# A two-block transformer on one core: another opening, own buffers for modulation weights, bias rows in 16 copies

## The chip, the cores and the metric

One Trainium2 chip, one of its cores, one launch. The metric is the device time of the launch in microseconds (us), the median of several runs. Data lies in the device's HBM at the start; every weight is read once.

## The reference, cut to what matters

Two blocks of two layers each work on x of 256 tokens by 1024 features, all in fp32. Only the parts that the change meets are written out.

```python
def first_block(x, c, ...):
    c_act = silu(c)                                   # 1 x 1024
    for l in range(2):
        mod = c_act @ w_ada[l] + b_ada[l]             # 6 x 1024: w_ada[l] is 1024 x 6144
        sh1, sc1, gt1, sh2, sc2, gt2 = split(mod, 6)
        h = rms_norm(x, norm_mix[l]) * (1 + sc1) + sh1
        p = h @ w_in[l]                               # all projections of the mixer
        # y_att: dilated attention; y_rwkv: a linear recurrence per head (8 heads);
        # y_gmlp: spatial gating with w_s, b_s
        merged = sum over the three of sigmoid(gates) * (y @ w_branch[l])
        x = x + gt1 * (merged @ w_out[l])
        h = rms_norm(x, norm_ffn[l]) * (1 + sc2) + sh2
        x = x + gt2 * conv_gated_ffn(h, ...)          # 1024 -> 2 x 2816 -> 1024
    return rms_norm(x, norm_final)

def second_block(x, p, rel_bias, ...):                # 2 layers: ffn1, mixer, ffn2, gated p @ w_pe_proj
    # the mixer's attention adds bias = rel_bias[t5_buckets(key - query)], 8 heads, window 128
```

## The kernel before

x is kept transposed: eight tiles of 128 features by 256 tokens. Every large product is made of three matmuls on a split into a high and a low part: each weight half (`raw`, 128 x 1024, 512 KB) is read by the sync queue (SP), cast to the high part by ScalarE (L137), and VectorE takes the difference as the low part (L138). `mm3` (L164 to L166) then does high x high, high x low, low x high. A call of `wload` reads one weight pair, two halves. The weight buffers stand in rings: 3 raw and 4 split ones for the whole program, and 3 and 2 or 3 and 3 more in the opening's pool `st` and the feed-forward's pool `wx`. Activations are split likewise (`split`, L201 and L202) into 17 buffers of pool `hp`.

The opening (`build`, L1340 on, and `LayerA.__init__`, L362 on): c is loaded as one row, spread to 128 partitions by a matmul, and scaled. x comes in eight loads on the sync queue. Weight pairs 12 and 6 follow, then the modulation weights of the first shift and scale, 16 blocks of 128 outputs by 1024 (six loads of 1 MB and four halves), with pair 10 before the last four halves. Each block's product with silu(c) is one VectorE operation that multiplies and sums along the row (L371). Meanwhile `rms` sums the squares of x on VectorE (L222), reduces them by one-column matmuls (L228), takes the root and reciprocal (L240, L241) and spreads the result (L248). `modulated` makes the eight h tiles: product with the norm on VectorE (L418), scale and shift on ScalarE (L419), split. `fmulti` then runs the three first weight pairs, k outermost, for all their columns; the second column of each sits in one of only two `aux` PSUM buffers.

The other 80 modulation blocks of 512 KB (`ada_task`, L337 load, L338 product) are called from a list, 0.67 of one at each `wload` (`tick`), and take the next raw buffer of the weight ring. The results are needed at the entries of mixers and feed-forwards and before their last products.

In the first feed-forward (`ffn_a`), after 8 of 22 weight pairs, `bias_rows` (L1004 on) makes 8 rows of 512 from `rel_bias` by a matmul and writes each 128 times to HBM (`skew`, L1018, on ScalarE's DMA queue). `bias_table` (L1023) reads it back at the start of the second block, shifted by one element from row to row, in two loads on SP; the second block's attention adds it (L1050). In the first feed-forward `project` (L1261 on) also does a small product of the second block and writes it to HBM in 256 KB pieces (L1285); it has four buffers of one tag.

The recurrence runs per pair of heads (`rwkv_pair`, generators that are advanced between weight pairs); the buffer counts of its tiles are in `BUFS`. The spatial gating's weights `w_s` have a tile of their own (`ws`, L886).

The kernel is written in a tile language. Its compile-time scheduler reorders what each engine and DMA queue is given: among the instructions whose inputs, by its own cost model, are ready and whose buffers are free, the first in program order goes next. On the chip each engine and queue then works strictly in that fixed order.

Of the kernel before, what the change touches and what calls it, by code (L numbers as in the profile page):

```python
# [17 lines left out]
S = 256  # L18
D = 1024
# [31 lines left out]
class K:  # L51
    def __init__(self, tc, ctx, ins):
# [4 lines left out]
        self.hp = E(tc.tile_pool(name="hp", bufs=17))  # L57
# [274 lines left out]
def ada_task(G, l, f, mods, cact):  # L332
    def run():
        nc = G.nc
        p, b = G.ring("raw")
        raw = p.tile([128, D], F32, tag="raw", bufs=b, name=G.nm("raw"))
        nc.sync.dma_start(raw, G.ins["w_ada"][l, f // 2, :, (f % 2) * D:(f % 2) * D + D])  # L337
        nc.vector.scalar_tensor_tensor(raw, raw, 1.0, cact, MUL, MUL, accum_out=mods[f // 8][:, f % 8:f % 8 + 1])  # L338
    return run


class LayerA:


    def __init__(self, G, l, pool, cact, first=None, late=None):
# [12 lines left out]
        else:  # L358

            for n, j in enumerate((0, 4, 1, 5, 2, 6, 3, 7)):  # L360
                if n == 6:
                    late()  # L362
                raw = first.tile([128, 2, D], F32, tag="ada", bufs=8, name=G.nm("raw"))
                src = v3(G.ins["w_ada"][l, j], 2)
                if n < 6:
                    nc.sync.dma_start(raw, src)
                for h in range(2):
                    if n >= 6:
                        nc.sync.dma_start(raw[:, h, :], src[:, h, :])
                    f = 2 * j + h  # L370
                    nc.vector.scalar_tensor_tensor(raw[:, h, :], raw[:, h, :], 1.0, cact, MUL, MUL, accum_out=self.mods[f // 8][:, f % 8:f % 8 + 1])  # L371
        G.bg += [((l, f), ada_task(G, l, f, self.mods, cact)) for f in range(0 if first is None else 16, 48)]
# [66 lines left out]
BUFS = dict(P=1, iP=1, kkn=1, kp=1, BK=1, AR=2, bv=2, uv=8, SA=1, SR=2, BT=2, AT=2, Q=4, R=1, X=1, Y=1, ST=2, y=2)  # L439


def rwkv_pair(G, L, mp, p, zk, zr, zv, zwa, sg, out, O):
# [80 lines left out]
    rkb = mp.tile([128, 128], F32, tag="rkb", name=G.nm("rkb"), bufs=2)  # L523
# [211 lines left out]
def mix_a(G, L, x, l, mp, pre, dbg=None):  # L735
# [81 lines left out]
    def gmlp_bias():  # L817
        tt(ws, ws, G.c("causal", 128).unsqueeze(1).to_broadcast([128, 8, 128]), MUL)
        yield 1.5
        for p in range(4):  # L820
            ps = G.aux()
            for g in range(2):
                mm(ps[64 * g:64 * g + 64, :128], G.ones[:, :64], ws[:, 2 * p + g, :], start=True, stop=True)
# [14 lines left out]
    def gmlp_out():  # L838
        for p in range(4):
            ps = G.aux()  # L840
            for t in range(2):
                for g in range(2):
                    mm(ps[64 * g:64 * g + 64, t * 128:t * 128 + 128], gv[t][:, (2 * p + g) * 64:(2 * p + g) * 64 + 64],
                       ws[:, 2 * p + g, :], start=True, stop=True)
# [41 lines left out]
    ws = mp.tile([128, 8, 128], F32, tag="ws", name=G.nm("ws"), bufs=1)  # L886
    nc.sync.dma_start(ws, G.ins["w_s"][l])
# [5 lines left out]
    start(3)  # L893
    heads(1)
# [679 lines left out]
```

## Time and profile before

| what | value |
|---|---|
| median of 3 runs | 2295.76 us (2294.28 to 2296.1) |
| the profiled execution | 2297.13 us |
| its span, from the first to the last instruction | 2295.3 us |
| TensorE (PE) busy | 2206.4 us, 96% |
| weight loads of TensorE (PEld) | 2131.8 us, 93% |
| VectorE (DVE) | 1685.2 us, 73% |
| ScalarE (ACT) | 1286.4 us, 56% |
| read from HBM | 408.40 MB |

A view groups or lists the instructions of that one execution; times count from the span's first instruction. "PE" are matmuls, "PEld" the weight loads that overlap them, "SPq" and "ACTq" what the queues of SyncE and ScalarE issue. L12 is line 12 of the kernel. An instruction's idle time is that of its engine just before it, with who ended it. Matmuls are pipelined: their listed durations overlap, and the distance of their starts tells the pace.

### The profile page before, as it was taken

What the parts mean: (1) busy time and instruction counts of PE and PEld (TensorE: products, weight loads), DVE (VectorE), ACT (ScalarE), POOL (GpSimd) and SP (SyncE); (2) the same over time, 40 slices, a digit from 0 to 9 for tenths busy, and PEclk for the clock granted to TensorE, in tenths of its full rate; (3) what the DMA queues carried; (4) which work ended last, traced back from release to release, by engine and by line L of the source; (5) the groups of instructions that cost most, each with busy time, mean ns of one, the idle gap of its engine ahead of it and who ended that gap; (6) DMA issues with size and microseconds to landing.
All of it is one profiled execution on the core that took longest, in us unless ns stands there. A gap on an engine that the chain in (4) does not pass through costs nothing.

```text
span 2295.3 us, 46372 instructions
## 1 busy us (share of the span) xinstructions
PE 2206.4 (96%) x18850; PEld 2131.8 (93%) x18850; DVE 1685.2 (73%) x3042; ACT 1286.4 (56%) x2184; POOL 4.2 (0%) x10
## 2 busy tenths in 40 slices
PE   5999998978999999999999999999999999999999
PEld 4889998978888999899999999999999999999999
DVE  6887777757678877776576569976677656997665
ACT  4575546544557554655454466664465446665444
POOL 0000000000000000000000000000000000000000
PEclk9999999989999999999999999999999999999999
DMA  7634457777563446765675663466565556346653
GB/s 289 200 121 150 148 192 256 224 220 231 179 188 122 150 150 190 262 213 156 176 238 170 173 196 109 140 216 184 158 209 182 171 175 194 102 149 214 184 159 124
DMA packets 129148, 416.66 MB, mean 182 GB/s; under 512 B 14596, under 2 KB 20356, under 8 KB 128166
## 3 DMA queue, kind: packets, MB, share of 16 engines
q1 hardware_dynamic: 126750, 409.50, 57.0%
q10 hardware_dynamic: 2184, 4.19, 1.0%
q8 instruction: 148, 2.42, 0.4%
q14 instruction: 66, 0.54, 0.1%
HBM read 408.40 MB, written 5.24 MB: 180 GB/s over the span
## 4 chain that ended last, share of the span: by engine, by line
PE 77%; DMA 9%; DVE 7%; ACT 5%; issue 1%; SPq 0%; ACTq 0%; DVEq 0%
PE ps L164 22%; PE ps L165 22%; PE ps L166 22%; DVE lo L138 3%; DMA skew<-ohb 2%; ACT hi L137 2%; DMA raw<-in_ffn_up 2%; DMA raw<-in_w_ada 2%; DMA raw<-in_w_in 1%; PE rec L601 1%; PE rec L593 1%; DVE raw L371 1%; DMA raw<-in_w_out 1%; PE rec L1182 1%; PE aux L1044 0%
## 5 line engine op out<-in xcount | busy, mean ns | idle before, releaser
L164 PE MATMUL ps<-h,hi 128*128 128x256 f32 x5080 | 1437.1, 284 | 31.0 <-ACT h L201 28.5
L166 PE MATMUL ps<-h,lo 128*128 128x256 f32 x5080 | 1433.2, 283 | 15.4 <-DVE lo L138 15.4
L165 PE MATMUL ps<-l,hi 128*128 128x256 f32 x5080 | 1432.2, 283 | 5.1 <-DVE l L202 5.0
L137 ACT CAST hi<-raw 128x1024 fp32r<-128x1024 f32 (+1 forms) x724 | 704.8, 977 | 640.2 <-PE ps L165 360.3
L138 DVE TENSOR_TENSOR lo<-raw,hi 128x1024 fp32r<-128x1024 f32 (+1 forms) x724 | 819.7, 1134 | 300.7 <-ACT hi L137 297.6
L164 PEld LDWEIGHTS ps<-h,hi 128*128 128x128 f32 x5080 | 959.7, 189 | 44.1 <-ACT h L201 30.8
L166 PEld LDWEIGHTS ps<-h,lo 128*128 128x128 f32 x5080 | 961.2, 189 | 21.0 <-DVE lo L138 16.8
L165 PEld LDWEIGHTS ps<-l,hi 128*128 128x128 f32 x5080 | 961.2, 189 | 11.2 <-DVE l L202 6.8
L201 ACT CAST h<-t 128x256 fp32r<-128x256 f32 x172 | 68.7, 403 | 126.1 <-DVE t L1000 96.2
L202 DVE TENSOR_TENSOR l<-t,h 128x256 fp32r<-128x256 f32 x172 | 72.5, 424 | 66.1 <-ACT h L201 65.7
L338 DVE SCALAR_TENSOR_TENSOR raw<-raw,cact 128x1024 f32<-128x1024 f32 x80 | 97.4, 1218 | 30.3 <-DMA raw<-in_w_ada 30.2
L997 DVE TENSOR_TENSOR t<-ps,r 128x512 f32<-128x512 f32 x88 | 60.8, 691 | 41.6 <-PE ps L166 41.2
L1187 DVE SCALAR_TENSOR_TENSOR cy<-cp,cwh,cy 128x256 f32<-128x256 f32 x192 | 85.2, 478 | 3.2 <-ACT cy L1185 2.9
L215 ACT ACTIVATE t<-x 128x256 f32<-128x256 f32 x96 | 38.5, 407 | 16.4 <-DVE x L968 9.1
L222 DVE TENSOR_TENSOR t<-t,t 128x256 f32<-128x256 f32 x87 | 36.6, 421 | 5.4 <-ACT t L215 4.1
L190 PE MATMUL ps<-hi,h 128*128 128x256 f32 x128 | 38.2, 299 | 0.0
L191 PE MATMUL ps<-hi,l 128*128 128x256 f32 x128 | 37.7, 294 | 0.0
L1000 DVE TENSOR_TENSOR t<-t,t 128x256 f32<-128x256 f32 x88 | 36.9, 420 | 1.0 <-ACT t L999 1.0
L192 PE MATMUL ps<-lo,h 128*128 128x256 f32 x128 | 37.4, 292 | 0.0
L999 ACT ACTIVATE t<-t 128x256 f32<-128x256 f32 x88 | 36.1, 411 | 0.9
L964 ACT ACTIVATE t<-t 128x256 f32<-128x256 f32 x44 | 18.1, 415 | 27.3 <-DVE t L963 27.0
L419 ACT ACTIVATE t<-t,sh,am 128x256 f32<-128x256 f32 x32 | 18.1, 596 | 26.5 <-DVE am L398 22.5
(312 smaller groups left out, 1890.3 us busy)
## 6 DMA issues: line engine op xcount, KB each, us to landing
raw<-in_w_in SPq DMA_DIRECT2D x176, 512.0 KB, 4.3
raw<-in_ffn_in SPq DMA_DIRECT2D x176, 512.0 KB, 4.5
raw<-in_ffn_up SPq DMA_DIRECT2D x88, 512.0 KB, 5.6
raw<-in_w_ada SPq DMA_DIRECT2D x84, 512.0 KB, 4.8
raw<-in_ffn_out SPq DMA_DIRECT2D x64, 384.0 KB, 3.1
raw<-in_ffn_out SPq DMA_DIRECT2D x64, 320.0 KB, 3.2
raw<-in_w_branch SPq DMA_DIRECT2D x24, 512.0 KB, 4.2
raw<-in_ffn_down SPq DMA_DIRECT2D x32, 384.0 KB, 3.1
```

Source lines behind the costliest of these rows:

```text
L137: nc.scalar.copy(hi[:, :m], raw[:, :m])
L138: nc.vector.tensor_tensor(lo[:, :m], raw[:, :m], hi[:, :m], SUB)
L164: mm(ps, w[0], x[0], start=first, stop=False)
L165: mm(ps, w[0], x[1], start=False, stop=False)
L166: mm(ps, w[1], x[0], start=False, stop=last)
L190: mm(ps[:, :256], x[k][0][:, sl], h, start=k == 0, stop=False)
L201: nc.scalar.copy(h, src)
L202: nc.vector.tensor_tensor(l, src, h, SUB)
L215: nc.scalar.square(sq, x[k])
L338: nc.vector.scalar_tensor_tensor(raw, raw, 1.0, cact, MUL, MUL, accum_out=mods[f // 8][:, f % 8:f % 8 + 1])
L997: nc.vector.tensor_tensor(v3(gu, 2), v3(ps, 2), rb, MUL)
L1187: stt(y, cp[:, jj:jj + S], cwh[:, jj * 4 + i:jj * 4 + i + 1], y, MUL, ADD)
```

## The change

The opening: silu(c) is loaded in 128 copies and as a column; x goes out on two queues; the 16 modulation blocks come one by one, scale block k and shift block k for k from 0 to 7, five of them in another layout for TensorE (8 matmuls of one column each), with the weight pairs 12, 6 and 10 after the second, fourth and last pair of blocks; all eight squares go to TensorE, which sums them. Later blocks get two buffers of their own. A block's load and its product are tied behind the instruction traced just before them on their engine (`keep_in_program_order`), and a product is traced only when the block after the next is called, or at a `need`. `modulated` puts the shift into the split, except in the opening. The bias rows are made in 16 copies as one 128 x 512 tile and written once; the table is read in 16 loads on GpSimd's queue. There are fewer buffers in some places: one less of `hp`, one less raw of the feed-forward, fewer in the recurrence (`BUFS`, `rkb`), and `ws` now takes two buffers of the z tiles.

```diff
-        self.hp = E(tc.tile_pool(name="hp", bufs=17))
+        self.hp = E(tc.tile_pool(name="hp", bufs=16))
...
+    def ada_flush(self, keep=0):
+        while len(self.ada_pend) > keep:
+            self.ada_pend.pop(0)()
...
+    def rms_pe(self, x):
+        ps = self.aux()
+        sqs = []
+        for k in range(8):
+            sq = self.tmp(S)
+            nc.scalar.square(sq, x[k])
+            sqs.append(sq)
+        self.load_ident()
+        for t in range(2):
+            for k, a in enumerate(sqs):
+                nc.tensor.matmul(ps[:, t:t + 1], a[:, t * 128:t * 128 + 128], self.ones[:, 0:1], start=k == 0, stop=k == 7)
+        return self.spread(self.inv_rms(ps[:, :2]), False)
...
-def ada_task(G, l, f, mods, cact):
+def ada_task(G, l, f, mods, cact, pool):
     def run():
-        p, b = G.ring("raw")
-        raw = p.tile([128, D], F32, tag="raw", bufs=b, name=G.nm("raw"))
-        nc.sync.dma_start(raw, G.ins["w_ada"][l, f // 2, :, (f % 2) * D:(f % 2) * D + D])
-        nc.vector.scalar_tensor_tensor(raw, raw, 1.0, cact, MUL, MUL, accum_out=mods[f // 8][:, f % 8:f % 8 + 1])
+        G.ada_flush(ADA_BUFS - 1)
+        raw = pool.tile([128, D], F32, tag="adar", bufs=ADA_BUFS, name=G.nm("ada"))
+        G.tc.keep_in_program_order(nc.sync.dma_start(raw, G.ins["w_ada"][l, f // 2, :, (f % 2) * D:(f % 2) * D + D]))
+        def product():
+            G.tc.keep_in_program_order(
+                nc.vector.scalar_tensor_tensor(raw, raw, 1.0, cact, MUL, MUL, accum_out=mods[f // 8][:, f % 8:f % 8 + 1]))
+        G.ada_pend.append(product)
...
-            for n, j in enumerate((0, 4, 1, 5, 2, 6, 3, 7)):
...
+            for k in range(8):
+                for f in (8 + k, k):
+                    raw = first.tile([128, D], F32, tag="ada", bufs=15, name=G.nm("raw"))
+                    out = self.mods[f // 8][:, f % 8:f % 8 + 1]
+                    if f in ADA_PE:                    # 0, 1, 2, 3, 5
+                        nc.sync.dma_start(raw, G.ins["w_ada_pe"][ADA_PE.index(f)])
+                        ps = G.rec()
+                        for i in range(8):
+                            nc.tensor.matmul(ps[:, 0:1], raw[:, i * 128:i * 128 + 128], ccol[:, i:i + 1], start=i == 0, stop=i == 7)
+                        nc.scalar.copy(out, ps[:, 0:1])
+                    else:
+                        nc.sync.dma_start(raw, G.ins["w_ada"][l, f // 2, :, (f % 2) * D:(f % 2) * D + D])
+                        nc.vector.scalar_tensor_tensor(raw, raw, 1.0, cact, MUL, MUL, accum_out=out)
+                late(k)                                # k 1, 3, 7: load_w of pairs 12, 6, 10
...
 def modulated(G, x, a, sh):
-        nc.vector.tensor_tensor(t, x[k], r, MUL)
-        nc.scalar.activation(t, t, AF.Identity, scale=a[:, k:k + 1], bias=sh[:, k:k + 1])
-        out.append(G.split(t))
+            nc.vector.scalar_tensor_tensor(t, x[k], a[:, k:k + 1], r, MUL, MUL)
+            h, l = (G.hp.tile([128, S], F32R, tag="h", name=G.nm("h")) for _ in range(2))
+            nc.scalar.activation(h, t, AF.Identity, bias=sh[:, k:k + 1])
+            nc.vector.scalar_tensor_tensor(l, t, sh[:, k:k + 1], h, ADD, SUB)
...
-BUFS = dict(P=1, iP=1, kkn=1, kp=1, BK=1, AR=2, bv=2, uv=8, SA=1, SR=2, BT=2, AT=2, Q=4, R=1, X=1, Y=1, ST=2, y=2)
+BUFS = dict(P=1, iP=1, kkn=1, kp=1, BK=1, AR=2, bv=2, uv=8, SA=1, SR=2, BT=2, AT=1, Q=3, R=1, X=1, Y=1, ST=2, y=1)
...
-    ws = mp.tile([128, 8, 128], F32, tag="ws", name=G.nm("ws"), bufs=1)
-    nc.sync.dma_start(ws, G.ins["w_s"][l])
+    wst = [mp.tile([128, 2, S], F32, tag="zkr", name=G.nm("ws"), bufs=3).rearrange("p a (b j) -> p (a b) j", b=2) for _ in range(2)]
+    for i in range(2):
+        nc.sync.dma_start(wst[i], G.ins["w_s"][l][:, 4 * i:4 * i + 4, :])
...
-    sk = G.dr.tile([8, 128, 512], F32, name="skew")
-    nc.tensor.matmul(ps[0:8, :], rel, oh, start=True, stop=True)
-    t = pool.tile([8, 512], F32, tag="ohb", name="ohb")
-    nc.scalar.dma_start(sk, t.unsqueeze(1).to_broadcast([8, 128, 512]))
+    sk = G.dr.tile([128, 512], F32, name="skew")
+    rel16 = pool.tile([33, 128], F32, tag="rel16", name="rel16")
+    nc.vector.tensor_copy(v3(rel16, 16), rel.unsqueeze(1).to_broadcast([33, 16, 8]))
+    nc.tensor.matmul(ps, rel16, oh, start=True, stop=True)
+    t = pool.tile([128, 512], F32, tag="pj", name="ohb", bufs=5)
+    nc.scalar.dma_start(sk, t)
...
     for q in range(2):
-        G.nc.sync.dma_start(bias[:, :, q, :], src)
+        for a in range(0, 128, 16):
+            src = bass.AP(tensor=sk.tensor, offset=sk.offset + 127 - a + (128 if q == 0 else 0), ap=[[8 * 512 - 1, 16], [512, 8], [1, 256]])
+            G.nc.gpsimd.dma_start(bias[a:a + 16, :, q, :], src)
...
-        return mp.tile([128, 512], dt, tag=tag, name=G.nm("pj"), bufs=4)
+        return mp.tile([128, 512], dt, tag=tag, name=G.nm("pj"), bufs=5 if tag == "pj" else 4)
...
-                nc.sync.dma_start(t, ins["x"][:, k, :])
+                G.tc.keep_in_program_order((nc.scalar if k % 2 else nc.sync).dma_start(t, ins["x"][:, k, :]))
...
-                        G.weights(wx, 3, 3)
+                        G.weights(wx, 2, 3)
```

## Rows read from the trace of the kernel before

**Rows 1.** Busy time by stage: stretch, its us, each engine's busy us (instructions), PEclk, DMA share, GB/s.

```profile
0.00:56.10 56.10, 27.43 (x160) 23.53 (x161) 38.55 (x90) 25.25 (x45) 2.29 (x7) 1.00 0.81 295
56.10:370.30 314.20, 304.25 (x2915) 281.20 (x2913) 252.12 (x549) 188.19 (x347) 0.96 (x1) 1.00 0.54 171
370.30:382.40 12.10, 8.59 (x59) 8.39 (x60) 7.20 (x15) 5.80 (x11) 0.00 (x0) 0.86 0.94 319
382.40:600.40 218.00, 195.97 (x1586) 192.78 (x1587) 151.32 (x251) 104.59 (x166) 0.00 (x0) 0.95 0.72 220
600.40:954.70 354.30, 337.77 (x3130) 314.43 (x3128) 273.57 (x585) 209.61 (x386) 0.99 (x2) 0.97 0.55 171
954.70:1144.70 190.00, 189.95 (x1601) 189.62 (x1601) 131.82 (x204) 107.54 (x176) 0.00 (x0) 1.00 0.60 185
1144.70:2295.30 1150.60, 1142.41 (x9404) 1121.81 (x9403) 830.63 (x1353) 645.43 (x1059) 0.00 (x0) 1.00 0.56 173
```

**Rows 2.** The same view of the opening, its first 10 us and the rest.

```profile
0.00:10.00 10.00, 3.78 (x4) 1.16 (x4) 2.73 (x9) 6.03 (x11) 1.16 (x5) 1.00 0.64 178
10.00:45.00 35.00, 15.08 (x89) 14.21 (x90) 30.42 (x67) 13.05 (x22) 0.00 (x0) 1.00 1.02 396
```

**Rows 3.** Groups by line, opening: operation, count, busy us, mean ns, idle before.

```profile
L371 DVE SCALAR_TENSOR_TENSOR raw<-raw,cact 128x1024 f32<-128x1024 f32 x16 | 19.0, 1220 | 0.0
L138 DVE TENSOR_TENSOR lo<-raw,hi 128x1024 fp32r<-128x1024 f32 x7 | 8.5, 1223 | 5.2 <-ACT hi L137 5.2
...
L419 ACT ACTIVATE t<-t,sh,am 128x256 f32<-128x256 f32 x8 | 4.5, 595 | 22.5 <-DVE am L398 22.5
```

**Rows 4.** Timeline of TensorE in the opening: start, us, instruction, idle before it.

```profile
30.29 0.58 PE L164 MATMUL ps<-h,hi 128*128 128x256 f32 x1 [13.67 <-ACT h L201]
...
35.73 0.41 PE L164 MATMUL aux<-h,hi 128*128 128x256 f32 x1
35.95 0.34 PE L165 MATMUL aux<-l,hi 128*128 128x256 f32 x1
...
55.99 0.28 PE L166 MATMUL aux<-h,lo 128*128 128x256 f32 x1
```

**Rows 5.** The chain that ended last, 425 to 550 us: start, us, what.

```profile
435.26 47.28 DMA skew<-ohb
...
524.10 4.75 DMA raw<-in_w_ada
```

**Rows 6.** Waits of TensorE, first feed-forward: us in total, times, longest.

```profile
PE ps L166 <- DVE lo L138: 14.0, 4, 7.3
PE ps L164 <- ACT h L201: 9.8, 3, 3.5
```

**Rows 7.** Line 228 in the opening: durations min/median/max ns, first and last start.

```profile
L228 PE MATMUL aux<-ones,t x8: 352/352/373, 10.1 to 11.6; 128*128 128x1 f32 x8
```

**Rows 8.** Waits of VectorE, and of the sync queue, whole span.

```profile
DVE raw L338 <- DMA raw<-in_w_ada: 30.2, 25, 4.0
...
SPq L337 <- DVE lo L138: 116.1, 42, 11.1
```

**Rows 9.** Timeline: feed-forward's tail (VectorE, TensorE), then its entry (VectorE, ScalarE).

```profile
528.88 1.23 DVE L338 SCALAR_TENSOR_TENSOR raw<-raw,cact 128x1024 f32<-128x1024 f32 x1 [1.91 <-DMA raw<-in_w_ada]
...
539.30 0.39 PE L164 MATMUL ps<-h,hi 128*128 128x256 f32 x1 [3.16 <-ACT h L201]
...
378.38 0.42 DVE L418 TENSOR_TENSOR t<-x,aux 128x256 f32<-128x256 f32 x1 [2.02 <-PE aux L248]
...
380.48 0.59 ACT L1284 COPY pj<-ps 128x512 f32<-128x512 f32 x1 [4.10 <-DMA proj<-pj]
```

**Rows 10.** Waits of TensorE, second mixer.

```profile
PE rec L262 <- ACT t L483: 2.5, 1, 2.5
```

**Rows 11.** Lines 669 and 521 in the first mixer: first and last start.

```profile
L669 DVE SCALAR_TENSOR_TENSOR yr<-y,vec,rec x4: 479/480/481, 175.8 to 322.8; 128x256 f32<-128x256 f32 x4
...
L521 DVE TENSOR_TENSOR t<-z,kp x4: 417/418/421, 73.1 to 233.6; 128x256 f32<-128x256 f32 x4
```

**Rows 12.** Line 1050: first and last start.

```profile
L1050 DVE SCALAR_TENSOR_TENSOR sc<-aux,bias x16: 680/683/692, 1408.8 to 2013.4; 128x512 f32<-128x512 f32 x16
```

More of the change, by code (lines that the diff above doesn't have):

```diff
@@ L358, in __init__ @@
         else:
-            for n, j in enumerate((0, 4, 1, 5, 2, 6, 3, 7)):
[L361 to L372, printed above, removed]
+            for k in range(8):
[12 more added lines that the diff above has]
+                late(k)
+        G.bg += [((l, f), ada_task(G, l, f, self.mods, cact, p)) for f in range(0 if first is None else 16, 48)]
     def load_small(self):
@@ L413, in modulated @@
     nc = G.nc
-    r = G.rms(x, False, True)
+    r, first = G.first_rms, G.first_rms is not None
+    G.first_rms = None
+    if not first:
+        r = G.rms(x, False, True)
     out = []
@@ L417, in modulated @@
         t = G.tmp(S)
-        nc.vector.tensor_tensor(t, x[k], r, MUL)
-        nc.scalar.activation(t, t, AF.Identity, scale=a[:, k:k + 1], bias=sh[:, k:k + 1])
-        out.append(G.split(t))
+        if first:
+            nc.vector.tensor_tensor(t, x[k], r, MUL)
+            nc.scalar.activation(t, t, AF.Identity, scale=a[:, k:k + 1], bias=sh[:, k:k + 1])
+            out.append(G.split(t))
+        else:
+            nc.vector.scalar_tensor_tensor(t, x[k], a[:, k:k + 1], r, MUL, MUL)
+            h, l = (G.hp.tile([128, S], F32R, tag="h", name=G.nm("h")) for _ in range(2))
+            nc.scalar.activation(h, t, AF.Identity, bias=sh[:, k:k + 1])
+            nc.vector.scalar_tensor_tensor(l, t, sh[:, k:k + 1], h, ADD, SUB)
+            out.append((h, l))
     return out
@@ L522, in rwkv_pair @@
     ps = G.rec()
-    rkb = mp.tile([128, 128], F32, tag="rkb", name=G.nm("rkb"), bufs=2)
+    rkb = mp.tile([128, 128], F32, tag="rkb", name=G.nm("rkb"), bufs=1)
     ts(rkb, G.c("blk", 128), 64.0, L.col("r_k", p), MUL, MUL)
@@ L817, in gmlp_bias @@
     def gmlp_bias():
-        tt(ws, ws, G.c("causal", 128).unsqueeze(1).to_broadcast([128, 8, 128]), MUL)
+        for w in wst:
+            tt(w, w, G.c("causal", 128).unsqueeze(1).to_broadcast([128, 4, 128]), MUL)
         yield 1.5
@@ L822, in gmlp_bias @@
             for g in range(2):
-                mm(ps[64 * g:64 * g + 64, :128], G.ones[:, :64], ws[:, 2 * p + g, :], start=True, stop=True)
+                mm(ps[64 * g:64 * g + 64, :128], G.ones[:, :64], wst[p // 2][:, 2 * (p % 2) + g, :], start=True, stop=True)
             yield 0.7
@@ L843, in gmlp_out @@
                     mm(ps[64 * g:64 * g + 64, t * 128:t * 128 + 128], gv[t][:, (2 * p + g) * 64:(2 * p + g) * 64 + 64],
[L844 removed]
+                       wst[p // 2][:, 2 * (p % 2) + g, :], start=True, stop=True)
             yield 0.8
@@ L1338, in build, with late @@
                     G.weights(sp, 3, 2)
-                    crow = sp.tile([1, D], F32, name="crow")
-                    nc.sync.dma_start(crow, ins["c"])
-                    nc.scalar.activation(crow, crow, AF.Silu)
-                    for i in range(2):
-                        ps = G.aux()
-                        nc.tensor.matmul(ps, G.ones[0:1, :], crow[:, i * 512:i * 512 + 512], start=True, stop=True)
-                        nc.scalar.activation(cact[:, i * 512:i * 512 + 512], ps, AF.Copy, scale=float(D))
-                    load_x()
-                    load_w(12)
-                    load_w(6)
-                    L = [LayerA(G, 0, lp, cact, sp, lambda: load_w(10))]
+                    ccol = sp.tile([128, 8], F32, name="ccol")
+                    nc.sync.dma_start(cact, ins["c"].to_broadcast([128, D]))
+                    load_x()
+                    G.tc.keep_in_program_order(nc.scalar.dma_start(ccol, ins["cc"]))
+                    nc.scalar.activation(ccol, ccol, AF.Silu)
+                    nc.scalar.activation(cact, cact, AF.Silu)
+                    def late(k):
+                        if k in (1, 3, 7):
+                            load_w({1: 12, 3: 6, 7: 10}[k])
+                    G.first_rms = G.rms_pe(x)
+                    L = [LayerA(G, 0, lp, cact, sp, late, ccol)]
                     G.wps.pop()
@@ L1511, in arrays @@
     out["c"] = i["c"]
+    out["w_ada_pe"] = np.stack([i["w_ada"][0][:, f * 128:f * 128 + 128].reshape(8, 128, 128).transpose(1, 0, 2).reshape(128, D) for f in ADA_PE])
+    out["cc"] = np.ascontiguousarray(_feat(i["c"][0]))
     out["w_ada"] = np.ascontiguousarray(i["w_ada"].reshape(L, D, 24, 2, 128).transpose(0, 2, 4, 3, 1)).reshape(L, 24, 128, 2048)
```

15 lines of the change are left out of this document (10 added, 5 removed).

## The prediction

> **What bounds the kernel now.** I read busy time by stage first, then the waits of TensorE, then the chain of waits where a stage loses time. By stage [rows 1] TensorE is idle 28.7 us in the opening (56.1 − 27.4), 10.0 in the rest of the first mixer, 3.5 at the entry of the first feed-forward, 22.0 in that feed-forward (218.0 − 196.0), 16.5 in the second mixer with its two entries, nothing in the second feed-forward, 8.2 in all that follows: 89 us. That, and the time in which it runs at the half clock, is all that can be won; the rest is matmuls that the change doesn't touch. The two feed-forwards run the same code on the same shapes: the second takes 190.0 us with TensorE never idle (0.119 us a matmul), the first 218.0. That pair is my yardstick.
>
> The opening is bound by two things at once. From 10 to 45 us the DMA engines are full, at 396 GB/s, and VectorE is busy 30.4 of those 35 us [rows 2]: 16 modulation products of 1.22 us (19.0) and seven splits of weights (8.5) [rows 3]. TensorE starts its first main matmul at 30.3 us after 13.7 us of waiting for h, and ends the three first weight pairs at 56.1 [rows 4].
>
> The first feed-forward is held up by the chain's longest piece, the 47.3 us write of the bias rows from 435 us on; a load of modulation weights, 4.8 us, follows in the chain at 524 us [rows 5]. In this stage TensorE waits 14.0 us for low parts of weights and 9.8 us for h [rows 6].
>
> **The change, part by part.**
>
> *Opening.* The same transfers come in another order. Up to the second half of weight pair 10 it moves cact's 128 copies (0.52 MB), x (1.05), vectors and identity (0.17), 16 modulation blocks (8.39) and three weight pairs (3.15): 13.28 MB. Before moves 178 GB/s x 10 us = 1.78 MB in its first 10 us [rows 2]; I keep that, since issue and x's small rows set it. The other 11.5 MB at 396 GB/s take 29.0 us: pair 10 is there at 39.0 us, the last modulation block, 1.05 MB ahead of it, at 36.4. In before, 1.5 MB of constants and small tables went among these.
>
> The Trainium skill (DMA: Bandwidth & Descriptors, section Where 436 GB/s comes from) has loads from HBM bound at about 358 GB/s. By that page the 11.5 MB would take 32.1 us, and the opening's gain below would be 3 us smaller. The trace holds 396 GB/s for 35 us, so the measurement decides, and this gets no chance of its own.
>
> VectorE does 11 products instead of 16 (−6.1 us) and no additions of squares, so it has some 24 us of work in that time, less than the transfers. TensorE takes over five blocks, 8 matmuls of one column each. One of these is two instructions, and eight instructions started from 10.1 to 11.6 us, 0.21 apart [rows 7]: 16 x 0.21 = 3.4 us a block, 17 in all. The mean square becomes 32 such instructions, 6.7 us instead of 1.7. The mean square and blocks 0 and 1 run where TensorE is idle; blocks 2, 3 and 5 stand among main matmuls. First h: x has landed by 10 us, the second half of the mean square takes 3.4 more, root and reciprocal about 2, spread 0.8, two blocks 6.8: 23, and columns, activation (0.6) and cast 1.4: main matmuls start near 24 instead of 30.3. From there to 39 us TensorE has 84 main matmuls (7 of 8 k for two pairs, 0.119 each: 10.0) and three blocks (10.2 at the half clock, 5.7 at 0.119) in 15 us: just enough, with up to 3 us left over. Last h: 36.4 + 1.2 product + 0.4 columns + 1.0 on ScalarE + 0.4 = 39.4; 12 matmuls to 40.8; pair 10's 48 to 46.5; with half of the leftover 48. Before: 56.1. That is 8; I take 7, as the order on each engine is fixed when the program is built, by times that need not be the chip's. Bounds: 9.6 won, or 6 lost (rival one).
>
> *Bias rows.* 2 MB out of 8 partitions become 256 KB out of 128. Even at the old rate that is 47.3/8 = 5.9 us. *Modulation loads.* In before VectorE stands still for them 30.2 us in 25 waits [rows 8]. At the feed-forward's tail one such wait (1.9 us) sits between parts of a gated value, and TensorE then waits 3.2 us for h at 539.3 [rows 9], the first of two. Now a product is traced one load later and pinned behind what VectorE was given just before, so its data should have landed. Together: the first feed-forward exceeds the second by 28.0 us, though it has 15 instructions fewer (1.8 us): 29.8, of which 22.0 idle and 7.8 half clock. Lower end: only the write's waits go, 14.0 [rows 6] and their share of the half clock (7.8 x 14/22 = 5.0), 19.0. Upper end 29.8. I take 25: the stage still carries modulation loads, which the second doesn't, and one refill at the change to the down projection may stay.
>
> The wait that is added: a modulation load on the sync queue waits until the product two blocks earlier is done on VectorE, and weight loads stand behind it. That queue already held these loads 116.1 us over 42 waits for a split [rows 8], 2.8 us each, while TensorE in the mixers lost almost nothing; and weights now keep their raw buffers to themselves, though the feed-forwards get two extra ones instead of three. I cost it at nothing; without that cover it is rival three.
>
> *Entry of the first feed-forward.* ScalarE waits 4.1 us for a buffer of the projection's write and gets on at 380.5 us, while VectorE's first product was there at 378.8 [rows 9]. A fifth buffer takes 2.0 of it away, from 0 (the next copy waits in its place) to 3.5, all the idle time there.
>
> *Shift inside the split.* At three entries one ScalarE activation of 0.60 us [rows 3] leaves the chain from the norm to h; VectorE's operation stays, with one more operand: 3 x 0.6 = 1.8 (0.5 to 3).
>
> *Second mixer.* TensorE waits 2.5 us for one ScalarE operation of a head pair [rows 10], shortly after a VectorE wait for a modulation block; I take 1.5 of it (0 to 4 with the half clock).
>
> *Smaller buffers.* AT, Q, y, rkb: four head pairs end between 175.8 and 322.8 us [rows 11], 49 us apart, and each of these tiles serves its own pair, so the next one finds it free: 0. The w_s halves now wait for z buffers of pairs 1 and 2, whose last reads lie between 73.1 and 233.6 us [rows 11]; if that holds up the sync queue, up to 2. One h buffer fewer: a first split waits for one more release wherever inputs change; I add 1.0 (0 to 3).
> *Bias table.* Sixteen loads on the POOL queue for two on SP, issued near the end of the second feed-forward at 1144.7 us and first read at 1408.8 [rows 12]; each could take 16 us: 0 (−1 to +1 for the sync queue that it leaves).
>
> Sum: −7 − 25 − 2 − 1.8 − 1.5 + 1 = −36.3. The profiled execution took 2297.1 us (the span, 2295.3, and 1.8 around it): 2260.8. The median shown is 1.4 below that execution: 2259.4, so **2260**.
>
> **Rivals.**
> *One: the opening keeps the half clock.* For: the mixer's first matmuls were still 0.22 us apart at 35.7 us, 5.4 us after their start [rows 4], and one-column products and waits for transfers now stand among them. Against: with no such work between, the spacing halved right after. Price: 144 x (0.21 − 0.12) = 13, so the opening loses 6: 2273.
> *Two: the pinned order changes little.* A product is pinned behind one instruction alone, so it may still be planned early. Then the feed-forward wins 19.0 and the second mixer nothing: 2267.
> *Three, slower: modulation loads starve the weights.* Place: the sync queue, where the load waits for a product and the next half of a weight behind it. Price: the product's 1.22 us for each of 80 loads, 98 us if none is covered. The time comes out above before once 36.3/98, 37% of the loads, make TensorE wait; at half of them: 2259.4 + 49 = 2308. For: VectorE is 80% busy in the mixers, so a product waits its turn. Against: the 2.8 us holds of before would show as idle time there, and don't.
> *Four, more:* the first feed-forward comes to the second's length (4.8) and the mixers lose 5 of their 26.5 idle us: 2250.
>
> **How the numbers follow.** Forecast 50% (its own range 2252 to 2268), one 18%, two 15%, three 7%, four 10%. What a measurement tells from no change is 0.2%, 4.6 us: below 2291 is faster. All but the third, and a bad form of the first, lie there: 0.91 faster, 0.03 within, 0.06 slower. The range reaches from the upper ends of opening, feed-forward, entry, split and second mixer together (2295.7 − 9.6 − 29.8 − 3.5 − 3 − 4 = 2246, less 2 for reordering) to rival one with the feed-forward's lower end (2273 + 6, and 4 for refills that I don't see): 2244 to 2283.
>
> **What would show it.** Right: the first main matmul near 24 us and pair 10's last near 48; no piece of the chain from the bias rows over 6 us; the first feed-forward at 190 to 197 us with under 6 us of idle; VectorE's waits for modulation loads under 5 us. Wrong: TensorE idle behind low parts of weights in the mixers while the sync queue waits for a product (three); spacing of 0.21 us well beyond 35 us (one); waits of 3 us again at the feed-forward's tail (two).

## The result, and the profile after

The kernel after takes 2268.76 us (median of 4 runs, 2265.74 to 2270.9), the one before 2295.02 beside it: ratio 0.989, 95% interval 0.9876 to 0.9904. The profiled execution took 2266.81 us, its span 2264.9, 30.4 less than before. The forecast was 2260 us. Busy time by stage, cut at the same main matmuls as [rows 1] (stretch, its us, each engine's busy us, PEclk, DMA share, GB/s):

```profile
0.00:68.20 68.20, 48.55 (x261) 47.02 (x262) 30.88 (x73) 24.10 (x49) 2.22 (x7) 0.95 0.68 243
68.20:381.40 313.20, 304.87 (x2915) 282.09 (x2913) 249.64 (x545) 186.82 (x345) 0.96 (x1) 1.00 0.52 172
381.40:390.65 9.25, 8.60 (x59) 8.40 (x60) 6.28 (x13) 5.17 (x8) 0.00 (x0) 0.82 0.85 267
390.65:580.50 189.85, 189.00 (x1586) 187.70 (x1587) 152.68 (x254) 103.46 (x160) 0.00 (x0) 1.00 0.77 253
580.50:923.20 342.70, 332.43 (x3130) 309.05 (x3129) 272.09 (x584) 203.76 (x374) 0.99 (x2) 0.99 0.53 172
923.20:1114.30 191.10, 190.50 (x1601) 189.83 (x1601) 136.04 (x212) 105.72 (x169) 0.58 (x1) 1.00 0.61 193
1114.30:2264.90 1150.60, 1141.47 (x9405) 1120.06 (x9403) 828.91 (x1354) 645.28 (x1059) 7.96 (x16) 1.00 0.56 173
```

Taken from [rows 1], the stages change by +12.1, −1.0, −2.85, −28.15, −11.6, +1.1 and 0: −30.4 us. The first feed-forward is now as long as the second. The opening, forecast to win 7 us, loses 12.1.

**The opening.** Its two stretches, against [rows 2]:

```profile
0.00:10.00 10.00, 0.71 (x4) 0.71 (x4) 0.71 (x9) 3.57 (x7) 1.15 (x5) 1.00 0.71 199
10.00:45.00 35.00, 29.83 (x139) 29.10 (x140) 16.42 (x34) 10.73 (x23) 0.00 (x0) 1.00 1.02 388
```

The transfers keep their pace (388 GB/s), but VectorE, busy 30.4 of these 35 us before, is busy 16.4: it has less to do and stands idle for the rest. TensorE instead is busy 29.8. Its timeline (start, us, operation, count, idle before and who ended it):

```profile
16.14 3.55 PE L397 MATMUL rec<-ccol,raw 128*128 128x1 f32 x16
19.55 1.20 PE L272 MATMUL aux<-ca,rc 128*128 128x128 f32 x4
20.55 3.41 PE L397 MATMUL rec<-ccol,raw 128*128 128x1 f32 x16
26.90 0.58 PE L173 MATMUL ps<-h,hi 128*128 128x256 f32 x1 [2.94 <-ACT h L210]
...
29.92 3.41 PE L397 MATMUL rec<-ccol,raw 128*128 128x1 f32 x16
...
34.19 3.41 PE L397 MATMUL rec<-ccol,raw 128*128 128x1 f32 x16
39.45 0.58 PE L173 MATMUL ps<-h,hi 128*128 128x256 f32 x1 [1.86 <-ACT h L210]
...
45.89 1.84 PE L397 MATMUL rec<-ccol,raw 128*128 128x1 f32 x16
```

Five blocks of 16 instructions stand in its fixed order, two ahead of the first main matmul and three among them. ScalarE copies each result out of PSUM. These copies and what comes behind them:

```profile
19.73 0.16 ACT L398 COPY mod<-rec 128x1 f32<-128x1 f32 x1 [3.15 <-PE rec L397]
24.00 0.16 ACT L398 COPY mod<-rec 128x1 f32<-128x1 f32 x1 [4.11 <-PE rec L397]
...
33.36 0.16 ACT L398 COPY mod<-rec 128x1 f32<-128x1 f32 x1 [5.26 <-PE rec L397]
37.63 0.16 ACT L398 COPY mod<-rec 128x1 f32<-128x1 f32 x1 [4.11 <-PE rec L397]
38.02 1.09 ACT L454 ACTIVATE t<-t,sh,am 128x256 f32<-128x256 f32 x2 [0.23 <-DVE sh L427]
39.02 0.39 ACT L210 CAST h<-t 128x256 fp32r<-128x256 f32 x1
39.31 1.04 ACT L141 CAST hi<-raw 128x1024 fp32r<-128x1024 f32 x1
...
47.77 0.16 ACT L398 COPY mod<-rec 128x1 f32<-128x1 f32 x1 [6.17 <-PE rec L397]
```

A copy of 0.16 us stands at the head of ScalarE's order for 3 to 6 us, 22.8 us in all, and the casts wait behind it. VectorE's shift columns (L427) wait for the copies, 9.2 us in three waits, the longest of them here:

```profile
37.82 0.16 DVE L427 TENSOR_TENSOR sh<-mod,vec 128x2 f32<-128x2 f32 x1 [5.53 <-ACT mod L398]
```

VectorE doesn't stand idle for want of data: the last modulation block lands at 37.4 us, near the 36.4 forecast, but VectorE's last product of the opening starts at 52.9. The Trainium skill (PSUM — Partial Sum Buffer, section Engine vs sequencer instructions) calls the queues of ScalarE and VectorE strict first-in, first-out; these rows agree (casts behind a copy that waits 5.26 us).

**The first feed-forward.** The bias rows' write (issue, count, KB, us to landing), all waits of TensorE in the stage (us, times, longest; before: [rows 6]), the modulation products of the whole program (count, busy, mean ns, idle before; before: [rows 8]) and the wait of their loads on SP:

```profile
skew<-ohb ACTq DMA_DIRECT2D x1, 256.0 KB, 5.8
```
```profile
PE ps L174 <- DVE h L461: 0.8, 1, 0.8
PE ps L173 <- ACT h L460: 0.6, 1, 0.6
```
```profile
L366 DVE SCALAR_TENSOR_TENSOR ada<-ada,cact 128x1024 f32<-128x1024 f32 x80 | 96.6, 1214 | 2.8 <-DMA ada<-in_w_ada 2.8
```
```profile
SPq L362 <- DVE ada L366: 53.6, 44, 2.7
```

The 47.3 us write of [rows 5] lands after 5.8 us. Of 28.15 us won, 21.2 are idle time (22.0 to 0.85) and 7.0 are busy time (195.97 to 189.00): in this stage the records grant the half clock for 20.5 us before and for none after. The second mixer with its entries wins 6.3 us of idle time and 5.3 of busy time in the same way. From 75 us on, and short of the last 5, the granted clock is at this lower level (1.2 GHz) for 10.2 us in two stretches; before, 47.8 us in eight.

### The profile page after: what moved, and what is told of

Read it like the earlier page. It is cut to its first block, busy times and chain, and to the rows that moved or that the text cites. A ratio compares the mean times of both kernels' runs of the same rounds, so it can differ in the third digit from the quotient of the medians.

```text
span 2264.9 us, 46602 instructions
## 1 busy us (share of the span) xinstructions
PE 2215.4 (98%) x18950; PEld 2144.1 (95%) x18950; DVE 1676.5 (74%) x3029; ACT 1274.3 (56%) x2162; POOL 12.7 (1%) x26
## 3 DMA queue, kind: packets, MB, share of 16 engines
HBM read 408.92 MB, written 3.41 MB: 182 GB/s over the span
## 4 chain that ended last, share of the span: by engine, by line
PE 83%; DVE 5%; ACT 4%; DMA 3%; issue 1%; ACTq 0%; DVEq 0%; SPq 0%
PE ps L173 24%; PE ps L174 24%; PE ps L175 23%; DVE lo L142 2%; ACT hi L141 1%; PE rec L643 1%; PE rec L635 1%; PE rec L1229 1%; PE ps L199 1%; PE ps L201 1%; DMA raw<-in_ffn_in 1%; PE ps L200 1%; DMA proj<-pj 1%; DMA raw<-in_w_in 1%; PE aux L1091 0%
## 5 line engine op out<-in xcount | busy, mean ns | idle before, releaser
L173 PE MATMUL ps<-h,hi 128*128 128x256 f32 x5080 | 1434.8, 284 | 13.7 <-ACT h L210 9.1
L174 PE MATMUL ps<-l,hi 128*128 128x256 f32 x4024 | 1131.3, 282 | 0.5 <-DVE l L214 0.4
L173 PEld LDWEIGHTS ps<-h,hi 128*128 128x128 f32 x5080 | 957.7, 189 | 26.3 <-ACT h L210 9.9
L174 PEld LDWEIGHTS ps<-l,hi 128*128 128x128 f32 x4024 | 760.0, 189 | 5.2 <-DVE l L214 2.3
L174 PE MATMUL ps<-h,hi 128*128 128x256 f32 x1056 | 298.4, 283 | 0.8 <-DVE h L461 0.8
L174 PEld LDWEIGHTS ps<-h,hi 128*128 128x128 f32 x1056 | 198.7, 188 | 2.3 <-DVE h L461 1.4
L210 ACT CAST h<-t 128x256 fp32r<-128x256 f32 x148 | 59.8, 405 | 131.0 <-DVE t L1044 89.7
L366 DVE SCALAR_TENSOR_TENSOR ada<-ada,cact 128x1024 f32<-128x1024 f32 x80 | 96.6, 1214 | 2.8 <-DMA ada<-in_w_ada 2.8
L211 DVE TENSOR_TENSOR l<-t,h 128x256 fp32r<-128x256 f32 x148 | 62.6, 424 | 48.5 <-ACT h L210 48.5
L1043 ACT ACTIVATE t<-t 128x256 f32<-128x256 f32 x88 | 36.2, 412 | 9.6 <-DVE t L1041 8.7
L638 ACT COPY Y<-rec 128x256 f32<-128x256 f32 x40 | 14.8, 370 | 27.2 <-PE rec L635 26.7
```

Of the source, the lines that this page charges most:

```text
L173: mm(ps, w[0], x[0], start=first, stop=False)
L174: mm(ps, w[0], x[1], start=False, stop=False)
L210: nc.scalar.copy(h, src)
L211: nc.vector.tensor_tensor(l, src, h, SUB)
```

## The experiments

For each kernel, when the n-th main matmul starts (us, profiled execution): the 1st; the 144th, the last of the three first weight pairs; the first (1729th) and last (3312th) of the first feed-forward, with the bias rows' write between the 2401st and the 2501st; the first of the second feed-forward (5041st). The ratio is to the kernel before, run beside it, with its 95% interval. The median of before in these groups of runs was 2295.0 us (after), 2291.5 (e1 to e4), 2294.8 (e5 to e8), 2292.6 (e9 to e11) and 2292.8 (e12), so a difference of two medians from different groups can be off by some 3 us; differences below are of medians, and where it matters the one by ratios stands beside. The start times are of one execution each, which isn't always a middle one: e9's is the slowest of four (2277.3 us), e3's the slowest of ten (2290.4), e4's 4.8 us below its median.

| kernel | 1 | 144 | 1729 | 2401 | 2501 | 3312 | 5041 | median us, ratio |
|---|---|---|---|---|---|---|---|---|
| before | 30.3 | 56.0 | 382.4 | 464.5 | 493.8 | 600.3 | 954.8 | 2295.0 |
| after | 26.9 | 68.1 | 390.6 | 473.2 | 485.1 | 580.4 | 923.2 | 2268.8, 0.989 (0.9876 to 0.9904) |
| e1 | 22.9 | 56.9 | 377.6 | 460.2 | 472.1 | 567.5 | 915.6 | 2260.7, 0.9863 (0.9844 to 0.9882) |
| e2 | 30.7 | 56.3 | 376.7 | 459.9 | 471.8 | 567.2 | 911.4 | 2255.2, 0.9844 (0.9828 to 0.986) |
| e5 | 27.2 | 65.0 | 384.9 | 467.5 | 479.4 | 574.7 | 920.3 | 2264.0, 0.9862 (0.9847 to 0.9877) |
| e9 | 29.6 | 73.5 | 396.4 | 482.0 | 493.9 | 589.3 | 932.4 | 2270.9, 0.9901 (0.9879 to 0.9924) |
| e12 | 25.8 | 59.3 | 380.2 | 466.4 | 478.3 | 573.6 | 915.9 | 2258.5, 0.9847 (0.983 to 0.9864) |
| e11 | 33.0 | 61.6 | 387.4 | 470.3 | 482.2 | 577.6 | 923.2 | 2263.4, 0.9869 (0.9834 to 0.9904) |
| e3 | 26.8 | 66.9 | 392.5 | 485.2 | 507.9 | 603.2 | 947.2 | 2285.7, 0.9974 (0.9962 to 0.9985) |
| e4 | 26.6 | 67.8 | 392.6 | 475.9 | 487.8 | 597.8 | 955.5 | 2298.8, 1.0032 (1.0015 to 1.0049) |
| e10 | 26.6 | 66.9 | 389.4 | 471.0 | 482.9 | 579.3 | 934.0 | 2279.3, 0.9945 (0.9929 to 0.9961) |
| e6 | 26.8 | 67.9 | 393.5 | 476.7 | 488.6 | 583.9 | 926.5 | 2269.8, 0.9898 (0.9872 to 0.9924) |
| e7 | 27.2 | 68.5 | 394.7 | 477.5 | 489.4 | 584.8 | 930.8 | 2269.6, 0.989 (0.9875 to 0.9905) |
| e8 | 27.1 | 67.4 | 390.7 | 471.9 | 483.8 | 579.2 | 925.6 | 2269.9, 0.9884 (0.9868 to 0.9901) |

### The opening

**e1: no blocks on TensorE.**

```diff
-ADA_PE = (0, 1, 2, 3, 5)
+ADA_PE = ()
```

> The kernel after, with all 16 modulation products of the opening on VectorE; loads, their order and the mean square on TensorE stay. Theory (the opening lost 12.2 us because the one-column blocks of shift columns 2, 3 and 5 stand among main matmuls in TensorE's fixed order at 3.4 us each, and because VectorE's later products stand behind operations that wait for these columns): without them the three first weight pairs end near 58 us instead of 68.1, and the time is 2258 to 2261 us. Rival (the transfers' new order, the one-column mean square and the half clock make the loss, the blocks don't): the pairs end at 65 us or later, 2266 us or more.

As the theory has it: the pairs end 11.2 us earlier and the median falls by 8.1 (6.2 by ratios), so the blocks make the loss. Of the lead, 12.9 us at the end of the first feed-forward, some 6 are lost again behind it, in places that the edit doesn't touch (the scheduler orders each kernel anew; what costs them isn't shown). VectorE is busy again, and its last product starts at 43.4 us, 9.5 earlier:

```profile
10.00:45.00 35.00, 22.42 (x107) 20.97 (x107) 29.19 (x63) 12.33 (x25) 0.00 (x0) 0.90 1.02 378
```

**e2: the opening of before in the kernel after.**

```diff
-            for k in range(8):
-                for f in (8 + k, k):
-                    raw = first.tile([128, D], F32, tag="ada", bufs=15, name=G.nm("raw"))
...
+            for n, j in enumerate((0, 4, 1, 5, 2, 6, 3, 7)):
+                raw = first.tile([128, 2, D], F32, tag="ada", bufs=7, name=G.nm("raw"))
...
-                    G.first_rms = G.rms_pe(x)
```

> The kernel after with the opening of before (loads of x on one queue, the row of c spread by a matmul, 1 MB modulation loads in seven buffers, 16 products on VectorE, mean square by VectorE's sums); all else as in after. Theory (the opening's loss is its own, and what comes behind doesn't hang on it): the pairs end at 56 us, 12.2 us less, 2256.6 us (2254 to 2259). Rival (the lag is partly regained behind the opening in either case, or the reordered loads of the first mixer want the new opening): 2261 us or more.

As the theory has it: 11.8 us less at the 144th matmul, kept to the end; 13.5 by the medians, 10.6 by ratios. At 2255.2 us this is the lowest median of all. Its interval lies below that of after, but overlaps those of e1 and e12.

**e5: only columns 0 and 1 on TensorE.**

```diff
-ADA_PE = (0, 1, 2, 3, 5)
+ADA_PE = (0, 1)
```

> The kernel after with shift columns 0 and 1 alone on TensorE; columns 2, 3 and 5 go to VectorE. Theory (what costs is the place: blocks among main matmuls; columns 0 and 1 are made while TensorE has nothing else): the first main matmul stays near 26 us, the three first weight pairs end at 55 to 58 us as without any block (56.9), and the time is 2255 to 2261 us. Rival (the cost goes with the number of blocks, 11.2 us for five): two of them cost 4.5 us, the pairs end at 61 us or later, the time is 2263 us or more.

The theory of the place fell: two blocks keep 8.1 of the 11.2 us, with no block among main matmuls. The number of blocks doesn't give it either: the rival's bounds were met, but its rule asked for 4.5. These two hold up the first h (27.2 us against 22.9 in e1), and VectorE is less busy than in e1:

```profile
10.00:45.00 35.00, 25.30 (x115) 23.36 (x115) 22.31 (x53) 10.87 (x23) 0.00 (x0) 1.00 1.03 393
```

So the question became how a block reaches VectorE.

**e9 and e12: blocks that nobody reads, with and without the copy.** Both keep all 16 products on VectorE as e1; TensorE makes five blocks besides. It makes them from a buffer that VectorE's product overwrites, so here, unlike in after, a block can only begin behind that product.

```diff
+                        if f in (0, 1, 2, 3, 5):
+                            ps = G.rec()
+                            for i in range(8):
+                                nc.tensor.matmul(ps[:, 0:1], raw[:, i * 128:i * 128 + 128], ccol[:, i:i + 1], start=i == 0, stop=i == 7)
+                            nc.scalar.copy(idle[:, f:f + 1], ps[:, 0:1])   # e9 only
```

> As with all 16 products on VectorE, and TensorE runs the 40 one-column matmuls of five blocks besides, on the product's leftovers, into a tile that nobody reads (extra work; the result doesn't hang on it). This separates the blocks' time on TensorE from VectorE's waits for their columns. Theory formed on the two-block run, which kept 8.2 of the 11.2 us (VectorE's work sets the opening's end, and it stood idle at the head of its queue behind columns and the spread norm that TensorE made late): VectorE stays near 29 us busy between 10 and 45 us, the three first pairs end at 57 to 61 us, 2259 to 2263 us. Rival (the one-column matmuls' own time in TensorE's queue, 3.4 us a block at the half clock): the pairs end at 65 us or later, 2266 us or more.

My theory missed: nobody needs these columns, and yet the pairs end at 73.5 us. But ScalarE's copies wait as in after (30.9 us in all against 22.8), and the activation for h stands right behind the last one (copies' group, then the timeline):

```profile
10.00:45.00 35.00, 26.81 (x119) 25.55 (x119) 17.85 (x38) 10.68 (x24) 0.00 (x0) 1.00 1.02 375
```
```profile
L407 ACT COPY idle<-rec 128x1 f32<-128x1 f32 x5 | 0.8, 159 | 30.9 <-PE rec L406 30.9
```
```profile
55.26 0.16 ACT L407 COPY idle<-rec 128x1 f32<-128x1 f32 x1 [10.43 <-PE rec L406]
55.31 1.09 ACT L460 ACTIVATE t<-t,sh,am 128x256 f32<-128x256 f32 x2
```

> As the run with blocks that nobody reads, without the five copies of their results on ScalarE; no other engine waits for a block now, only TensorE itself makes them. Theory (in that run the copies stood at the head of ScalarE's fixed order for 4 to 10 us each, and the casts and activations behind them handed the blocks' delay on to h and to VectorE): the three first weight pairs end at 58 to 63 us instead of 73.6, VectorE is busy 25 us or more between 10 and 45 us, 2258 to 2264 us. Rival (the blocks' own time in TensorE's queue, ahead of the spread norm and among the main matmuls at the half clock, is enough): the pairs end at 67 us or later, 2266 us or more.

As the theory has it: without the five copies, 0.8 us of work, the pairs end 14.2 us earlier, though TensorE still makes the same 80 instructions (the medians differ by 12.4):

```profile
10.00:45.00 35.00, 30.70 (x149) 30.14 (x148) 27.62 (x63) 11.90 (x23) 0.00 (x0) 1.00 1.02 380
```
```profile
L405 PE MATMUL rec<-ccol,raw 128*128 128x1 f32 x80 | 15.9, 329 | 4.3 <-DVE raw L401 4.3
```

The blocks' own 15.9 us on TensorE cost 2.4 us (59.3 against 56.9). What e9 loses beyond that comes with the copies, whose wait ScalarE's order hands on to casts and activations.

**e11: three products on GpSimd.**

```diff
+                    if f in (2, 4, 6):
+                        nc.gpsimd.tensor_tensor(raw[:, h, :], raw[:, h, :], cact, MUL)
+                        nc.scalar.activation(raw[:, h, :], raw[:, h, :], AF.Copy, accum_out=self.mods[f // 8][:, f % 8:f % 8 + 1])
+                    else:
```

> The kernel after with the opening of before, in which shift columns 2, 4 and 6 are made by a multiplication on GpSimd and a sum along the row on ScalarE instead of VectorE's product. Theory (VectorE's work sets the opening's end): three products of 1.2 us less, the pairs end at 52 to 54 us instead of 56.3, 2250 to 2253 us against 2255.2. Rival (the order fixed in advance and GpSimd's own speed decide): the pairs end at 56 us or later, 2255 us or more.

Nothing won (61.6 us at the 144th against e2's 56.3, runs spread from 2250.6 to 2268.5 us), for a reason that I had not named. VectorE, then GpSimd, at the same time:

```profile
23.13 3.36 DVE L404 SCALAR_TENSOR_TENSOR raw<-raw,cact 128x1024 f32<-128x1024 f32 x1
...
28.29 3.11 DVE L404 SCALAR_TENSOR_TENSOR raw<-raw,cact 128x1024 f32<-128x1024 f32 x1
...
34.54 2.33 DVE L430 TENSOR_TENSOR am<-mod,vec 128x2 f32<-128x2 f32 x1
```
```profile
23.07 2.33 POOL L401 TENSOR_TENSOR raw<-raw,cact 128x1024 f32<-128x1024 f32 x1 [21.38 <-DMA raw<-in_w_ada]
...
34.30 2.54 POOL L401 TENSOR_TENSOR raw<-raw,cact 128x1024 f32<-128x1024 f32 x1 [3.98 <-DMA raw<-in_w_ada]
```

The 13 products left on VectorE take 19.5 us, as much as 16 took (19.0 in [rows 3]). So this didn't take work off VectorE, and doesn't decide the theory.

### The first feed-forward and the second mixer

**e3: bias rows in one copy as before,** with the table read in two loads on SP.

```diff
-    sk = G.dr.tile([128, 512], F32, name="skew")
+    sk = G.dr.tile([8, 128, 512], F32, name="skew")
...
-    nc.tensor.matmul(ps, rel16, oh, start=True, stop=True)
+    nc.tensor.matmul(ps[0:8, :], rel, oh, start=True, stop=True)
...
-    nc.scalar.dma_start(sk, t)
+    nc.scalar.dma_start(sk, t.unsqueeze(1).to_broadcast([8, 128, 512]))
```

> The kernel after with the bias rows as before: 8 rows, each written 128 times in one write, and the table read in two loads on the sync queue. Theory (the step of 17.5 us that lies between the 2400th and the 2500th main matmul is the write's alone): 17.5 us more, 2286 us (2283 to 2289), and TensorE waits some 14 us for low parts in the first feed-forward. Rival (the modulation loads' own buffers already spare part of that wait): 6 to 12 us more, 2275 to 2281 us.

16.9 us more by the medians (19.3 by ratios), as the theory has it. TensorE waits 8.3 us for low parts of weights and 5.9 for a high part. In the profile the feed-forward is 20.9 us longer (210.7 against 189.8 from the 1729th to the 3312th), 10.8 of it between the 2401st and 2501st and 5.7 in the hundred ahead of them. Another 3.4 us lie in its first 72 matmuls, before the write: TensorE waits 2.1 us for an h at 397.0 us, whose activation stands on ScalarE behind a copy that waits 2.6 us for the projection's write, and the records grant the lower clock level for 3.4 us from 396.7 on.

**e4: the modulation loads in the weight ring as before, and e10: the same with the two buffers given to the ring.**

```diff
-        raw = pool.tile([128, D], F32, tag="adar", bufs=ADA_BUFS, name=G.nm("ada"))
+        p, b = G.ring("raw")
+        raw = p.tile([128, D], F32, tag="raw", bufs=b, name=G.nm("raw"))
...
+                G.wps.append((lp, 2, 0))   # e10 only
```

> The kernel after with the later modulation loads as before: they take the next raw buffer of the weight ring, and load and product are placed freely. Theory (loads and products tied to program order won 9.8 us at the tail of the first feed-forward and some 8 us in the second mixer): 16 to 20 us more, 2285 to 2289 us, with waits for h of 3 us again at that tail. Rival two of the prediction (the pinned order changes little): under 5 us more, at most 2274 us.

> Modulation loads in the weight ring as before, placed freely, but the ring has the two buffers more that the own buffers took. Theory (what costs is that a weight load must wait for the product of a modulation block in its buffer, however many there are): 2285 to 2299 us, with waits for h at the tail of the first feed-forward. Rival (the number of raw buffers in flight is all): 2266 to 2274 us.

30.0 us more than after in e4, beyond both expectations and slower than before the change; 10.6 more in e10 (32.6 and 12.6 by ratios). So two buffers more in the ring are worth 19.5 us, and the buffers of their own 10.6 more: neither theory of e10 holds alone. The stages tell the two apart. The two buffers bring the first feed-forward from 205.2 us back to 189.8 (1729th to 3312th), after's length, and from there to the second feed-forward e10 still takes 12.0 us more than after. In the shared ring weight loads on SP (L137) wait for products of modulation blocks (us, times, longest; e4, then e10), and in after none does:

```profile
SPq L137 <- DVE raw L362: 84.3, 35, 5.4
```
```profile
SPq L137 <- DVE raw L362: 58.8, 25, 5.6
```

VectorE waits for the data alike in both:

```profile
L362 DVE SCALAR_TENSOR_TENSOR raw<-raw,cact 128x1024 f32<-128x1024 f32 x80 | 97.6, 1220 | 58.5 <-DMA raw<-in_w_ada 58.3
```
```profile
L362 DVE SCALAR_TENSOR_TENSOR raw<-raw,cact 128x1024 f32<-128x1024 f32 x80 | 97.7, 1221 | 59.2 <-DMA raw<-in_w_ada 59.1
```

**e6: own buffers, not tied to program order; e7: each product also traced right behind its load.**

```diff
-        G.tc.keep_in_program_order(nc.sync.dma_start(raw, G.ins["w_ada"][l, f // 2, :, (f % 2) * D:(f % 2) * D + D]))
+        nc.sync.dma_start(raw, G.ins["w_ada"][l, f // 2, :, (f % 2) * D:(f % 2) * D + D])
...
-        G.ada_pend.append(product)
+        product()   # e7 only
```

> The kernel after with load and product of the later modulation blocks not tied to program order; own buffers and the product traced one load later stay. Theory (the tie to program order won the tail of the first feed-forward and the second mixer): VectorE waits for these loads for 20 us or more again, TensorE waits for h at that tail, and the time is 2283 to 2290 us. Rival (the own buffers alone do it, since weights no longer share their ring): VectorE waits under 8 us, and the time is 2266 to 2274 us.

> The kernel after with own buffers for the later modulation blocks alone: each product is traced right behind its load, and nothing is tied. Theory (tie and later tracing count): as without the tie or worse, 2283 to 2295 us. Rival (own buffers alone do it): 2266 to 2274 us.

By their times both rivals hold, but e6's rival also had VectorE wait under 8 us. It waits 18.2 us again in e6, and the median moves by 1.0 us, which can't be told from nothing:

```profile
L365 DVE SCALAR_TENSOR_TENSOR ada<-ada,cact 128x1024 f32<-128x1024 f32 x80 | 97.3, 1218 | 18.3 <-DMA ada<-in_w_ada 18.2
```

**e8: the shift ahead of the split, as before.**

```diff
-        if first:
+        if True:
             nc.vector.tensor_tensor(t, x[k], r, MUL)
```

> The kernel after with scale and shift in one operation of ScalarE ahead of the split at every entry, as before. Theory (one operation of 0.6 us leaves the chain from the norm to h at three entries): 0.5 to 3 us more, 2269 to 2272 us, and the first main matmul after each of these three norms comes 0.6 us later. Rival (VectorE's operation with one more operand takes as long as what it spares): no difference beyond 1 us at these entries.

The medians differ by 1.1 us, inside the runs' spread. The waits for the first h show it at two of the entries, in after and then in e8:

```profile
390.65 0.39 PE L173 MATMUL ps<-h,hi 128*128 128x256 f32 x1 [0.65 <-ACT h L460]
...
586.58 0.58 PE L173 MATMUL ps<-h,hi 128*128 128x256 f32 x1 [1.11 <-ACT h L460]
```
```profile
390.71 0.39 PE L173 MATMUL ps<-h,hi 128*128 128x256 f32 x1 [1.47 <-ACT h L210]
...
586.15 0.58 PE L173 MATMUL ps<-h,hi 128*128 128x256 f32 x1 [1.94 <-ACT h L210]
```

0.82 and 0.83 us less for the first h, and 0.82 (0.41 against 1.23) at the second feed-forward. But after waits a second time in both feed-forwards, where e8 doesn't: 0.80 us for the low part at 392.1 (L461, the first of the two waits shown above), and 0.55 us for an h at 926.6. That leaves 0.0, 0.83 and 0.27.

## Why the prediction was right or wrong

The time came out 8.8 us above the forecast, inside the range, but as a sum of errors of both signs, and that it came so near is luck: in the profiles the opening missed by 19.1 us, and the second mixer with its entries (8.9 better) and the first feed-forward (3.15 better) made up most of it.

- *Opening, −7 forecast, +12.1 measured, outside the bounds (−9.6 to +6).* The step that failed is "it has some 24 us of work in that time, less than the transfers": I took TensorE's five blocks off VectorE and let every engine work as its data came. The durations were right (3.4 us a block, 6.99 us for the mean square, transfers at 388 GB/s, the last block there at 37.4 us). The order was what counted: the blocks' results pass through copies at the head of ScalarE's fixed order, and h and VectorE's remaining products stand behind them (e9 against e12). I had priced the copies at their 0.16 us and not asked what waits behind them. That this chain is all of after's 11.2 us isn't shown: there VectorE itself also waits for the copied columns (9.2 us), in e9 a block waits for VectorE's product besides, and another engine for the copies wasn't tried. By the figure that the prediction cites from the Trainium skill (DMA: Bandwidth & Descriptors, section Where 436 GB/s comes from), loads would have stayed under 358 GB/s; this trace too goes beyond it, with 388.
- *Rival one* put the opening's danger at the half clock, 13 us; the forecast itself priced the main matmuls at 0.119 us from 24 us on. The half clock did last: the blocks' 16 instructions take 3.41 us from 34.2 us and 1.84 from 45.9, and the records grant the full clock (2.4 GHz) from 44.0 us, against 36.1 before, and take it back for 3.4 us at 50.8 and again at 57.7. (PEclk reads 1.00 for 10 to 45 us, as no record lies ahead of these; the spacing tells the clock there.) But e12, with the full clock only from 43.5 us (and then without a break), ends its pairs at 59.3: the clock isn't the main cause.
- *First feed-forward, −25 forecast, −28.15 measured,* near the upper end of 29.8: rival four's first half came true. The write was forecast at 5.9 us by its bytes and took 5.8.
- *The pinned order* got the credit for the modulation loads. It does what I said to VectorE's waits (30.2 us in [rows 8], 18.2 without it, 2.8 with it), but TensorE doesn't feel those (e6, e7). The own buffers do it: two more buffers, and weight loads that no longer wait behind a product (e4, e10).
- *Second mixer with its entries, −1.5 and two shifts of 0.6 forecast, −11.6 measured.* Undersized: I counted one wait of 2.5 us [rows 10] and not the ring that weights and modulation loads shared. From the end of the first feed-forward to the start of the second, e4 takes 14.9 us more than after (357.7 against 342.8), e10 12.0.
- *Entry, −2.0 and one shift forecast, −2.85 measured. Shift inside the split:* 1.1 us at three entries against 1.8, as two of them wait again (e8). *Bias table:* forecast 0; the stage that reads it is 1150.6 us before and after. *Rival three, starved weights:* SP holds modulation loads for a product 53.6 us, 1.2 each; TensorE's waits for low parts of weights in the two mixers are 0.6 and 0.8 us.

The undone parts don't add up: −13.5 (e2), +16.9 (e3) and +30.0 (e4) would make the change worth 33.4 us where the medians give 26.3 (41.3 against 25.2 by ratios). One reason is in e4 itself: it goes back to the shared ring, but with two extra raw buffers in the feed-forwards where before had three, so it undoes more than the change did. Whether the write's waits and the ring's also cover each other isn't shown.

## What to carry to other kernels

Before work goes to an idle engine, follow its result through every fixed order that it enters: a tiny copy that waits for a slow producer holds all that is queued behind it, and the engine that was to be relieved may stand idle. Where loads of one kind held up another in a shared ring, more buffers won most here (19.5 us), then buffers of their own (10.6); where the loads stand in the program made no difference that the medians can tell. A wait is worth what the bounding engine feels of it: 15 us more of VectorE's waits moved the median by 1.0.

## What the runs showed of the hardware

In e11 GpSimd's multiplication and VectorE's operations on two SBUF operands excluded each other. A product that started 0.06 us after a multiplication of GpSimd's of 2.33 us took 3.36 us instead of 1.22, and an addition of 128 x 2 elements, 0.15 us elsewhere, took 2.33. The Trainium skill (SBUF — State Buffer, section SBUF: two separate sides) has the two share a port pair that one instruction holds to its end, the other fully blocked; e11's rows agree.

In e12 TensorE was busy 30.7 of 35 us from 10 us on, two thirds of it with one-column matmuls; it made 16 of their instructions in 3.41 us at 34.0 us, and the records grant the full clock from 43.5. In before, where main matmuls alone ran from 30.3 us, they grant it from 36.1. At the lower level a one-column instruction took as long (0.21 us) as a main matmul of 256 columns (0.22 in [rows 4]).
